# One row of one buffer stored on fifteen DMA engines: a layer-norm and GELU kernel bound by its transfers

## Chip, cores and metric

One core of a Trainium2 chip. The metric is the time of one execution on the device in microseconds (us), the median of several runs. The times compared here are of fast runs; label and label2 are single runs whose state is unknown, and are used for their traces alone. "Before" is the kernel as it stood, "the changed kernel" is it with the diff below. Engines in the profile: PE (TensorE), DVE (VectorE), ACT (ScalarE), POOL (GpSimd), SP (SyncE); "ACTq" and "SPq" are the sequencers of ACT and SP, where DMAs are issued. "DMA engine" is always one of the 16 that move data. No view of the profile numbers them. Numbers are names here: 15 ("the 16th") is the engine that gets no packet of the row from the transfer of 120 partitions, 0 and 1 are the two that get those of the transfers of two.

## Reference

```python
x: (8, 1024, 2048) float32; gamma, beta: (2048,)
normalized = (x - mean) / sqrt(var + eps)        # over the last axis
out = gamma * normalized + beta
return 0.5 * out * (1 + tanh(sqrt(2 / pi) * (out + 0.044715 * out ** 3)))
```

The input is 67.1 MB and so is the output. Each is moved once.

## The kernel before

The 8192 rows are cut into 16 buffers of 4 MB: 128 partitions, four rows of 8 KB each, which lie side by side in memory, so a partition's part of a buffer is one run of 32 KB. Five slots hold buffers. SP issues the loads; a load waits until the store that used its slot has landed. ACT issues the stores, a whole buffer at a time after its last row, the last buffer row by row.

```python
R = 4
SLOTS = 5
...
    xts = [sb(f"xt{s}", [P, R, d], f32) for s in range(SLOTS)]
...
    def slot(b):
        return (b + SLOTS - 1) % SLOTS
    def by_row(b):
        return b == B - 1
    def stored(b):
        return sum(16 * (R if by_row(c) else 1) for c in range(b) if slot(c) == slot(b))
...
            @block.sync
            def _(sy):
                for b in range(B):
                    s = slot(b)
                    if stored(b):
                        sy.wait_ge(s_store[s], stored(b))
                    ...
                    if b:
                        sy.dma_start(out=xts[s], in_=xg[b]).then_inc(s_load[s], 16)
...
            # ACT, for each row i after its GELU
                    if by_row(b):
                        ins.then_inc(s_r, 1)
                        ac.dma_start(out=og[b, :, q:q + 1], in_=xt[:, q:q + 1])._wait_ge(
                            s_r, b + q + 1).then_inc(s_store[slot(b)], 16)
                        ac.sem_inc(s_g, 1)
                    elif q == R - 1:
                        ins.then_inc(s_r, 1)
                        ac.dma_start(out=og[b], in_=xt)._wait_ge(s_r, b + 1).then_inc(s_store[slot(b)], 16)
                        ac.sem_inc(s_g, 1)
```

## Time and profile before

| | before |
|---|---|
| time, median of 3 runs | 319.68 us (319.67 to 319.75) |
| span in the profile | 317.8 us |
| moved | 134.27 MB, 423 GB/s in the mean |

These come from the page and the timed runs. The engines' sequences of packets are not a view of the profile: the trace holds a record of each packet (queue, start, duration, size) without the number of its engine, and I linked each packet to the one that starts where another ends, on the assumption, which no view shows, that every engine handles the packets of each transfer in order. For the kernel before this gives sixteen sequences of 348 packets each. The lines of the profile that carry the argument stand in the prediction.

### The profile page before, as it was taken

The numbers are of one execution on the slowest core, as the hardware profiler recorded it, in microseconds if no ns is written. First come the engines' busy times: TensorE is split into PE (matmuls) and PEld (weight loads), VectorE is DVE, ScalarE is ACT, GpSimd is POOL, SyncE is SP. The second block draws the span as 40 slices with busy tenths as digits, with TensorE's granted clock in tenths as the row PEclk, the third lists the DMA queues.
The fourth block names the chain that finished last, engine by engine and source line by source line (L and its number), as shares of the span: only waits on it lengthen the run. The fifth ranks groups of instructions, "written<-read, shape, count | busy, mean of one in ns | idle before, by whom it ended". The sixth has DMA issues, their size and how long they took to land.

```text
span 317.8 us, 2075 instructions
## 1 busy us (share of the span) xinstructions
PE 244.3 (77%) x520; PEld 57.1 (18%) x520; DVE 265.0 (83%) x514; ACT 253.9 (80%) x132; POOL 79.0 (25%) x73
## 2 busy tenths in 40 slices
PE   2769988888888898888877868598595895868810
PEld 1211222111212122211111111122121111112100
DVE  3499999999999999999969799696996969879500
ACT  2679999999999999999969779696995969968920
POOL 1033323232323231323213222231312213212000
DMA  7999999999999999999999999999999999999994
GB/s 291 438 462 396 459 396 445 412 454 404 458 400 459 422 437 445 412 450 408 458 417 441 437 421 454 404 458 412 450 433 425 450 408 450 408 458 421 437 404 206
DMA packets 5571, 134.27 MB, mean 423 GB/s; under 512 B 656, under 2 KB 704, under 8 KB 704
## 3 DMA queue, kind: packets, MB, share of 16 engines
q1 hardware_dynamic: 2736, 67.11, 49.4%
q10 hardware_dynamic: 2832, 67.13, 49.1%
q14 instruction: 3, 0.02, 0.0%
HBM read 67.13 MB, written 67.11 MB: 422 GB/s over the span
## 4 chain that ended last, share of the span: by engine, by line
DMA 44%; DVE 27%; ACT 19%; PE 3%; issue 2%; ACTq 1%; DVEq 0%; SPq 0%
DMA out_dram<-xt 27%; DVE sts L148 15%; DMA xt<-in_x_dram 15%; ACT yk L201 12%; DVE zg L164 9%; ACT xt L208 7%; PE ps L226 2%; DMA rows<-in_gamma_dram 2%; DVE mvs L157 2%; DVE nms L141 1%; ACTq L216 1%; DVE ves L158 1%; PE ps L243 1%; ACT g_t L197 1%; ACTq L211 0%
## 5 line engine op out<-in xcount | busy, mean ns | idle before, releaser
L148 DVE BATCH_NORM_STATS2 sts<-xt 128x6 f32<-128x512 f32 x256 | 163.5, 681 | 23.7 <-DMA xt<-in_x_dram 21.7
L201 ACT ACTIVATE yk<-xt,nms,rss 128x2048 bf16<-128x2048 f32 x64 | 134.1, 2095 | 41.7 <-DVE nms L141 41.2
L243 PE MATMUL ps<-zg,ident 128*128 128x512 bf16 x256 | 120.8, 627 | 50.9 <-DVE zg L164 50.9
L132 POOL TENSOR_TENSOR rss<-ves,mhalf 128x1 f32<-128x1 f32 x64 | 78.0, 1219 | 216.5 <-DVE ves L158 157.0
L239 PE MATMUL ps<-b_hl,ones_b 33*128 33x512 bf16 x256 | 120.6, 624 | 2.2 <-PEq L234 2.2
L208 ACT ACTIVATE xt<-ps 128x2048 f32<-128x2048 f32 x64 | 118.8, 1857 | 1.5 <-PE ps L243 1.5
L164 DVE TENSOR_TENSOR zg<-yk,g_t 128x2048 bf16<-128x2048 bf16 x64 | 78.0, 1218 | 5.0 <-ACT yk L201 3.0
L243 PEld LDWEIGHTS ps<-zg,ident 128*128 128x128 bf16 x256 | 27.6, 130 | 144.1 <-DVE zg L164 108.7
L239 PEld LDWEIGHTS ps<-b_hl,ones_b 33*128 33x128 bf16 x256 | 27.0, 127 | 92.1 <-issue 88.4
L157 DVE BATCH_NORM_AGGREGATE mvs<-sts 128x2 f32<-128x24 f32 x64 | 16.9, 264 | 2.2
L141 DVE TENSOR_SCALAR nms<-mvs,rss 128x1 f32<-128x1 f32 x64 | 12.6, 196 | 0.0
L226 PE MATMUL ps<-rows,ones 1*128 1x512 f32 x8 | 7.2, 1072 | 6.0 <-DMA rows<-in_gamma_dram 6.0
L158 DVE TENSOR_SCALAR ves<-mvs 128x1 f32<-128x1 f32 x64 | 9.8, 154 | 2.2
L194 ACT ACTIVATE b_hl<-rows 1x2048 bf16<-1x2048 f32 x1 | 1.9, 1909 | 4.9 <-DMA rows<-in_beta_dram 4.9
L226 PEld LDWEIGHTS ps<-rows,ones 1*128 1x128 f32 x8 | 2.5, 323 | 9.2 <-DMA rows<-in_gamma_dram 6.0
L172 DVE TENSOR_TENSOR b_hl<-rows,b_hl 1x2048 bf16<-1x2048 f32 x1 | 2.3, 2281 | 2.1 <-ACT b_hl L195 2.1
L197 ACT ACTIVATE g_t<-ps 128x2048 bf16<-128x2048 f32 x1 | 1.9, 1877 | 2.4 <-PE ps L226 2.4
L190 ACT ACT_TABLE_LOAD x1 | 1.3, 1283 | 0.9 <-SPq L106 0.9
L167 DVE MEMSET b_hl<- 33x1024 uint32 x1 | 0.9, 912 | 1.2 <-SPq L106 1.2
L195 ACT ACTIVATE b_hl<-rows 1x2048 bf16<-1x2048 f32 x1 | 1.9, 1908 | 0.0
L123 POOL MEMSET ones<- 65x128 f32 x1 | 0.2, 202 | 0.5 <-SPq L106 0.5
L127 POOL TENSOR_SCALAR_AFFINE_SELECT ident<-ident 128x128 bf16<-128x128 bf16 x1 | 0.3, 294 | 0.1
(7 smaller groups left out, 0.9 us busy)
## 6 DMA issues: line engine op xcount, KB each, us to landing
xt<-in_x_dram SPq DMA_DIRECT2D x15, 4096.0 KB, 24.3
out_dram<-xt ACTq DMA_DIRECT2D x15, 4096.0 KB, 37.0
xt<-in_x_dram SPq DMA_DIRECT2D x4, 1024.0 KB, 8.1
out_dram<-xt ACTq DMA_DIRECT2D x4, 1024.0 KB, 12.7
rows<-in_beta_dram ACTq DMA_DIRECT2D x2, 8.0 KB, 5.6
rows<-in_gamma_dram ACTq DMA_DIRECT2D x1, 8.0 KB, 5.0
```

The source lines that it names most:

```text
L132: po.tensor_tensor(out=rss[:, c], in0=ves[:, c], in1=mhalf, op=ALU.pow)._wait_ge(s_a, k + 1).then_inc(s_q, 1)
L141: ve.tensor_scalar(out=nms[:, c], in0=mvs[:, q, 0:1], scalar1=rss[:, c], scalar2=-1.0, op0=ALU.mult, op1=ALU.mult)._wait_ge(s_q, count).th ...
L148: ins = ve.bn_stats(out=sts[:, q, j, :], in_=xr[:, j, :])
L157: ve.bn_aggr(out=mvs[:, q], in_=sts[:, q])._wait_ge(s_o, count + 1).then_inc(s_o, 1)
L158: ve.tensor_scalar(out=ves[:, q:q + 1], in0=mvs[:, q, 1:2], scalar1=float(eps), scalar2=1.0, op0=ALU.add, op1=ALU.mult)._wait_ge(s_o, coun ...
L164: ve.tensor_tensor(out=zgs[q % 2], in0=yks[q % 2], in1=g_t, op=ALU.mult)._wait_ge(s_n, count).then_inc(s_z, 1)
L197: ac.activation(out=g_t, in_=pss[0], func=ACT.Identity)._wait_ge(s_tg, 1).then_inc(s_c, 1)
L201: ac.activation(out=yks[t % 2], in_=xts[slot(b)][:, q], func=ACT.Identity, scale=rss[:, q:q + 1], bias=nms[:, q:q + 1])._wait_ge(s_p, t + ...
L208: ins = ac.activation(out=xt[:, q], in_=pss[i % 2], func=ACT.Gelu_apprx_tanh)._wait_ge(s_t, i + 1)
L226: ins = pe.matmul(pss[0][:, cols(j)], lhsT=ones[64:65], rhs=rows[64:65, j * K // nsub:(j + 1) * K // nsub, :d // K], start=True, stop=True)
L239: ins = pe.matmul(ps[:, cols(j)], lhsT=ones_b, rhs=b_hl[:, cols(j)], start=True, stop=False)
L243: ins = pe.matmul(ps[:, cols(j)], lhsT=ident, rhs=zgs[k % 2][:, cols(j)], start=False, stop=True)
```

## The change

Its intent, as its words say: relieve the 16th DMA engine of one row of one buffer. Row 3 of buffer 7 is stored for partitions 0 to 119 in one transfer, and for the other eight in four transfers of two partitions. The first three rows of that buffer go in one store ahead of it. The diff also changes the last buffer: rows 0 and 1 go together, where each row had a store.

```diff
+LIGHT = 7
...
-    def by_row(b):
-        return b == B - 1
+    def stores(b):
+        every = slice(0, P)
+        if b == B - 1:
+            return [(0, 2, [every]), (2, 3, [every]), (3, 4, [every])]
+        if b == LIGHT:
+            return [(0, 3, [every]), (3, 4, [slice(0, 120)] + [slice(120 + a, P, 4) for a in range(4)])]
+        return [(0, R, [every])]
...
+                    for p in groups:
+                        ac.dma_start(out=og[b, p, lo:hi], in_=xt[p, lo:hi])._wait_ge(s_r, count).then_inc(
+                            s_store[slot(b)], 16)
+                    ac.sem_inc(s_g, 1)
```

The semaphore targets (`stored`) and the count of `s_r` follow from the same list.

More of the change, by code (lines that the diff above doesn't have):

```diff
@@ L98, in cols @@
         return slice(j * FMAX, (j + 1) * FMAX)
-    def by_row(b):
-        return b == B - 1
+    def stores(b):
[5 more added lines that the diff above has]
+        return [(0, R, [every])]
     def stored(b):
-        return sum(16 * (R if by_row(c) else 1) for c in range(b) if slot(c) == slot(b))
+        return sum(16 * len(p) for c in range(b) if slot(c) == slot(b) for _, _, p in stores(c))
     with tc.tile_critical(no_gpsimd_drain=True):
@@ L197, in _ @@
                 ac.activation(out=g_t, in_=pss[0], func=ACT.Identity)._wait_ge(s_tg, 1).then_inc(s_c, 1)
+                count = 0
                 for t in range(T + 1):
@@ L208, in _ @@
                     ins = ac.activation(out=xt[:, q], in_=pss[i % 2], func=ACT.Gelu_apprx_tanh)._wait_ge(s_t, i + 1)
-                    if by_row(b):
-                        ins.then_inc(s_r, 1)
-                        ac.dma_start(out=og[b, :, q:q + 1], in_=xt[:, q:q + 1])._wait_ge(
-                            s_r, b + q + 1).then_inc(s_store[slot(b)], 16)
-                        ac.sem_inc(s_g, 1)
-                    elif q == R - 1:
-                        ins.then_inc(s_r, 1)
-                        ac.dma_start(out=og[b], in_=xt)._wait_ge(s_r, b + 1).then_inc(s_store[slot(b)], 16)
-                        ac.sem_inc(s_g, 1)
-                    else:
-                        ins.then_inc(s_g, 1)
+                    ready = [g for g in stores(b) if g[1] == q + 1]
+                    if not ready:
+                        ins.then_inc(s_g, 1)
+                        continue
+                    count += 1
+                    ins.then_inc(s_r, 1)
+                    lo, hi, groups = ready[0]
+                    for p in groups:
+                        ac.dma_start(out=og[b, p, lo:hi], in_=xt[p, lo:hi])._wait_ge(s_r, count).then_inc(
+                            s_store[slot(b)], 16)
+                    ac.sem_inc(s_g, 1)
             @block.tensor
```

## The prediction

Four passages are cut from it where marked, because no run or trace of this case showed what they say: a paragraph on the number of engines in a transfer and on engines in general, how the odd transfers could come to run slowly, a fourth rival about instructions, and a word beside the last sign. That 120 partitions use 15 engines and two use two was assumed in steps 1 to 3.

> **What bounds the kernel now.** I read the page's DMA rows first, then its DMA queues, then the waits, the landings of the stores, and last the packet and semaphore records that lie under these views.
>
> The busy rows of the page, in 40 slices of 7.95 us:
>
> ```profile
> DVE  3499999999999999999969799696996969879500
> ACT  2679999999999999999969779696995969968920
> DMA  7999999999999999999999999999999999999994
> GB/s 291 438 462 396 459 396 445 412 454 404 458 400 459 422 437 445 412 450 408 458 417 441 437 421 454 404 458 412 450 433 425 450 408 450 408 458 421 437 404 206
> ...
> q1 hardware_dynamic: 2736, 67.11, 49.4%
> q10 hardware_dynamic: 2832, 67.13, 49.1%
> ```
>
> DVE and ACT are nearly full for the first half (digits of 9) and then show 6s and 7s; the DMA row is 9 from the second slice to the last but one. The two queues (loads, then stores; the columns are packets, MB and share of 16 engines' span) fill 98.5% together. So the transfers bound the kernel; compute has slack from half-way on. The waits of the load queue and of the rest say the same:
>
> ```profile
> DVE sts L148 <- DMA xt<-in_x_dram: 21.7, 8, 3.7
> ```
>
> ```profile
> SPq L119 <- DMA out_dram<-xt: 247.1, 11, 55.6
> ```
>
> The load queue waits 247 us for stores to free a slot, and DVE waits 21.7 us for loads. Nothing ahead of the DMA engines holds them up. At the end:
>
> ```profile
> 305.32 0.34 ACTq L211 DMA_DIRECT2D out_dram<-xt  x1
> ```
>
> This, from the timeline, is the issue of the last row's store. It lands at 316.5 us, 11.2 us later; the span ends at 317.8. The kernel ends when the slowest of the 16 engines has worked off its queue, and the shares above, being means over engines, cannot say by how much that one lags. The semaphore records can: each store counts 16, once for each engine. I read these times of its sixteen increments straight from the trace (us):
>
> ```
> buffer 0, issued  36.4: 14 engines 59.4 to 59.7,   then  59.9,  60.7
> buffer 6, issued 136.7: 14 engines 174.4 to 175.0, then 176.9, 178.3
> last row, issued 305.3: 14 engines 313.7 to 314.2, then 316.4, 316.5
> ```
>
> Two engines lag, not one. Linking each packet to the one that starts where another ends gives sixteen engines' sequences, without their numbers, about 8.39 MB each. None is left without a packet for more than about 0.3 us after 2 us. In the final rows an 8 KB packet follows the last every 0.306 us (26.8 GB/s), a 32 KB one takes 1.213 us. Fourteen sequences end at 313.3 to 313.9 us, two at 316.05 and 316.06. They lag for different reasons:
> - The **creeping engine** needs a mean of 1.2255 us for each 32 KB packet after 45 us where an ordinary engine needs 1.213; 213 such packets x 12.5 ns = 2.7 us. It falls behind steadily.
> - The **interrupted engine** is ordinary but for a few events. At 34.3 and at 99.5 us an 8 KB packet of the instruction queue takes 0.31 to 0.33 us, and the packet after it 1.875 and 1.744 us instead of 1.213: 0.32 + 0.66 + 0.31 + 0.53 = 1.8 us. Stretched packets at 60.4, 78.8 and 139.1 us (1.451, 1.347 and 1.395 us) add 0.24 + 0.13 + 0.18. In all 2.4 us, most of it before 140 us. (A third such fetch, at 109.9 us, seems to fall on another engine that ends 0.4 us late.)
>
> [...]
>
> **The change part by part.**
> 1. Row 3 of buffer 7 by 120 partitions: engine 15 (the 16th) is spared 8 packets of 8 KB, 8 x 0.306 = 2.45 us. The others keep their 8. This is just the lag of one of the two slow engines.
> 2. The other 8 partitions in four transfers of two: if each goes to engines 0 and 1, those get 4 packets more each, 4 x 0.306 = 1.22 us. If they are ordinary they end at 313.5 + 1.2 = 314.7 us, still ahead of a laggard's 316.06.
> 3. Buffer 7 in 24 KB and 8 KB pieces in place of 32 KB: 4 x 0.306 = 1.224 against 1.213 per partition, at most 8 x 0.011 = 0.09 us an engine; five more small semaphore packets of 9 ns on engines 0 and 1 (one more on the ordinary ones), under 0.05 us. The store of three rows is issued about a row (4.3 us) earlier than the whole was (153.4 us), but into a queue that already has work, since that buffer's store lands at 193.7 to 197.6 us: nothing gained.
> 4. The last buffer: rows 0 and 1 in one store instead of two. Row 0 was issued at 293.3 and waits until 297.6 now. The store of the buffer before, issued at 288.9, holds the engines to 303.9 us, so the delay is hidden. One semaphore packet and 8 packet boundaries fewer: less than 0.1 us gained.
> 5. ACT issues five more DMAs for buffer 7 and one fewer for the last: 4 x 0.34 = 1.4 us of its sequencer. ACT waits 41.2 us for DVE in all and the queues stay filled, so 0 on the path.
>
> Sum on the path: the 16th engine ends 2.4 us earlier if it is one of the two laggards. The end is then set by the other, at 316.05 instead of 316.06 us. The step 3 and 4 terms are within 0.1 us of each other. So I expect a gain of 0, give or take 0.2 us, out of a hoped-for 2.45, and 319.6 us (319.7 before, and 0.1 off for the one chance in six below).
>
> **The rivals.**
> - *The 16th engine is the only laggard that matters* (the change's intent). Then the end moves to the next slowest, engines 0 and 1 at about 314.7 us: 1.3 us earlier, 318.3 us. For it: the unprofiled runs might not have the second lag, if profiling makes it. Against: the profiled run took 319.58 us and the others 319.67 to 319.75, so the profile seems to add nothing; and both lags stand in the records of the last four stores. One chance in six.
> - *The extra packets fall on the other laggard*, that is, it is engine 0 or 1. Then it ends 1.22 us later, near 320.9 us. Nothing in the trace numbers the engines; with 2 of 15 engines, one chance in seven.
> - *The odd transfers run slowly*[...]. The disturbance would last as long as that row, 2.45 us at most, and hits engines with 2.2 us to spare, but the other laggard has none. Some tenths: 320.0 to 320.5 us. One in seven.
> - [...]
>
> **Range and chances.** The middle is no change, 319.7, set to 319.6 for the larger weight of the favourable side. The favourable rival gives 318.3 and the unfavourable 320.9; a range of 318.2 to 320.9 just holds both, and leaves out the gain of the whole 2.45 us (317.3) and two bad rivals at once, a tenth on each side. Two per cent is 6.4 us. To win that, all engines would have to move less data, and the bytes are the same; to lose it, the engines would have to run empty, and every queue has work waiting. So 0.98 for within 2%.
>
> **What would show it right or wrong.** Right: in the changed profile the last store still has a late increment, about 2.2 us behind the main group, but one in place of two; two engines end about 1.2 us after the ordinary ones; the last row's store is issued near 305.3 and the span is within 0.3 us of 317.8. Buffer 7's row has one 120-partition transfer with 15 increments by the DMA engines, and four with two. Wrong: all sixteen increments of the last store within 1.3 us of each other (the intent's gain), a last increment past 317 us (extra packets on the laggard), still two laggards as late as now (the 16th engine was neither), or more than 0.3 us of stretched packets around 195 us[...].

## The result, and the profile after

| | before | changed |
|---|---|---|
| time, median | 319.76 us (319.67 to 320.09, 6 runs) | 321.36 us (320.71 to 321.81, 6 runs) |
| ratio | | 1.0047, 95% interval 1.0034 to 1.0060 |
| span in the profile | 317.8 us | 319.3 us |
| last store's sixteen increments | 313.7 to 316.5 us | 314.8 to 318.0 us |

This ratio is the mean of the fast runs of one kernel over that of the other; the ratios of the experiments below come out of the fast runs of the same rounds without the first one, which was profiled. So they are not quite the ratios of the medians quoted. The change is 1.6 us slower. That is within 2%, as given 0.98, but above the range of 318.2 to 320.9.

The rows of the page of the changed kernel that answer to those of before:

```profile
DVE  3499999999999999999599899990596997969810
ACT  2679999999999999998599799991495996969960
...
DMA  7999999999999999999999999999999999999995
GB/s 293 433 452 427 428 402 447 406 452 423 435 447 407 448 419 443 443 415 447 415 443 439 417 449 397 416 390 431 427 447 431 431 423 431 447 435 423 423 414 223
...
q1 hardware_dynamic: 2736, 67.11, 49.4%
q10 hardware_dynamic: 2839, 67.13, 49.1%
```

The DMA row is as full as before and the bytes are the same, so the engines were not idle: some packets took longer. The GB/s row shows where: 397, 416 and 390 in the slices from 192 to 216 us (a slice is 8 us), where before has 454, 404 and 458. The number of packets on the store queue settles how the row was divided. It rose by 7, from 2832 to 2839. The data packets are as many as before; one store of 16 engines fewer in the last buffer takes away 16 small semaphore packets (656 for 41 transfers before), so the odd row added 23, which is 15 for the transfer of 120 partitions and 4 x 2 for the others, as the prediction assumed. (The trace has 39 packets of 4 bytes on that queue from 191 to 201 us: 16 of the three rows' store and these 23.)

The waits, for all engines and for the load queue:

```profile
DVE sts L155 <- DMA xt<-in_x_dram: 23.7, 6, 10.9
```

```profile
SPq L126 <- DMA out_dram<-xt: 247.5, 11, 54.9
```

The totals are hardly changed (21.7 and 247.1 us before). But one wait of DVE for a load is 10.9 us long, where 3.7 was the longest. The timeline tells which: the load of buffer 12 is issued when the store of buffer 7 has landed. In the changed kernel:

```profile
200.69 0.33 SPq L126 DMA_DIRECT2D xt<-in_x_dram  x1
```

and before:

```profile
197.66 0.33 SPq L119 DMA_DIRECT2D xt<-in_x_dram  x1
```

The buffer whose row was split lands 3 us later, although its first three rows were issued 4 us earlier. The issue of that row on ACT, in the changed kernel, with the issue of the last row of all:

```profile
153.76 3.23 ACTq L225 DMA_DIRECT2D out_dram<-xt  x5
...
310.06 0.34 ACTq L225 DMA_DIRECT2D out_dram<-xt  x1
```

Five issues took 3.23 us, 0.58 to 0.70 us each against 0.338 us for a store of 128 partitions (the two of 64 in halves7, below, took 0.55 and 0.60), and the last row's store comes at 310.1 us instead of 305.3.

Where did the 1.6 us come from? Busy time and GB/s in four stretches. The columns that matter are the last three: granted clock, DMA share, GB/s. Before:

```profile
186.00:196.00 10.00, 7.43 (x17) 1.73 (x18) 9.71 (x20) 9.24 (x6) 3.47 (x3) 1.00 1.04 449
196.00:201.00 5.00, 4.58 (x11) 1.18 (x12) 3.97 (x8) 4.28 (x3) 1.46 (x1) 1.00 1.05 452
201.00:208.00 7.00, 3.91 (x10) 0.92 (x9) 5.31 (x11) 4.27 (x3) 1.46 (x1) 1.00 0.93 403
208.00:216.00 8.00, 6.95 (x16) 1.56 (x15) 7.74 (x17) 7.29 (x4) 2.02 (x2) 1.00 1.03 442
```

Changed:

```profile
186.00:196.00 10.00, 8.20 (x18) 1.99 (x19) 9.74 (x20) 8.99 (x6) 3.12 (x3) 1.00 0.99 424
196.00:201.00 5.00, 4.58 (x11) 1.00 (x9) 4.93 (x10) 4.74 (x3) 1.46 (x1) 1.00 1.06 437
201.00:208.00 7.00, 6.17 (x15) 1.44 (x15) 6.86 (x14) 6.74 (x4) 2.92 (x2) 1.00 1.00 393
208.00:216.00 8.00, 6.97 (x16) 1.54 (x14) 7.70 (x16) 7.27 (x4) 1.64 (x2) 1.00 1.02 401
```

A packet counts whole where it starts, so a single stretch wobbles by some per cent (a share of 1.04 shows that). Over all 30 us it is 437 GB/s before and 413 after (each GB/s times its length, summed and divided by 30). The 24 GB/s that are missing over 30 us are 0.72 MB, which at 426 GB/s take 1.7 us: the whole loss of the kernel lies between 186 and 216 us.

The packet records show its form. After 45 us, a packet of 32 KB usually takes 1213 ns and one of 8 KB 309 ns. I call a packet stretched if it took over 50 ns more, and add up the excess over all engines. Before: 1.4 us. Changed: 25.5 us, 3.2 us of it in nine 8 KB packets of the odd row at 196.9 to 199.6 us (387 to 987 ns instead of 309), and 22.3 us in 52 packets of 32 KB, nearly all between 203 and 213 us. These are packets of ordinary transfers, the store of a later buffer and the load of buffer 12. Divided by 16 engines the 25.5 us are 1.6 us each.

In the linked sequences of the changed kernel the two with four more packets, engines 0 and 1, end last, at 317.7 and 316.9 us. The one without the row ends at 314.6 and takes 1.213 us for a 32 KB packet nearly throughout, so the 16th engine is neither the creeping nor the interrupted one. These two end at about 316.3 and 316.5, the rest between 314.5 and 316.0.

### The profile page after: what moved, and what is told of

Its sections match the earlier page's. It is cut to its first block, busy times and chain, and to the rows that moved or that the text cites. A ratio compares the mean times of both kernels' runs of the same rounds, so it can differ in the third digit from the quotient of the medians.

```text
span 319.3 us, 2079 instructions
## 1 busy us (share of the span) xinstructions
PE 244.3 (77%) x520; PEld 57.1 (18%) x520; DVE 265.0 (83%) x514; ACT 253.9 (80%) x132; POOL 79.1 (25%) x73
## 4 chain that ended last, share of the span: by engine, by line
DMA 45%; DVE 27%; ACT 19%; PE 3%; issue 2%; ACTq 1%; DVEq 0%; SPq 0%
DMA out_dram<-xt 27%; DMA xt<-in_x_dram 17%; DVE sts L155 16%; ACT yk L209 12%; DVE zg L171 9%; ACT xt L216 6%; PE ps L234 2%; DMA rows<-in_gamma_dram 2%; DVE mvs L164 2%; DVE nms L148 1%; ACTq L225 1%; DVE ves L165 1%; PE ps L251 1%; ACT g_t L204 1%; DVEq L185 0%
```

## The experiments

What is cut from the expectations below said which engines and partitions a transfer uses, or by what means packets would stretch; no run shows it. The theories, as they came up:
- **Theory 1, dry load queue:** the split row makes the store land late, the next load is issued late into an empty queue, and when loads come back all packets stretch.
- **Theory 2, heavy engines:** what costs is the four odd transfers on engines 0 and 1.
- **Theory 3, other division:** a row that isn't stored in one transfer of 128 partitions makes packets stretch. By what means was a guess of mine; no record shows which engine takes which partitions.
- **Theory 4, unequal loads:** packets stretch because engines have unequal work.
- **Theory 5:** theory 3 for the row itself; the later wave in ordinary 32 KB packets needs the late load as well.

All kernels but drop_eight gave the reference's result. The stretch is that of the one profiled run of each, which the ratio leaves out; runs of one kernel can differ by up to 5 us. halves7_late11 had one slow run of six, which is left out, and its interval reaches beyond 2%.

| kernel | median (us) | ratio | 95% interval | stretched 32 KB / 8 KB packets, us in all |
|---|---|---|---|---|
| before | 319.64 to 319.76 | 1 | | 1.4 / 0 |
| changed | 321.36 | 1.0047 | 1.0034 to 1.0060 | 22.3 / 3.2 |
| tail_only | 319.97 | 1.0008 | 0.9995 to 1.0022 | 0.9 / 0 |
| light7_old_tail | 321.37 | 1.0056 | 1.0042 to 1.0070 | 22.4 / 1.8 |
| split_only | 319.90 | 1.0007 | 0.9994 to 1.0021 | 7.6 / 0 |
| drop_eight | 320.27 | 1.0030 | 1.0017 to 1.0043 | 21.6 / 3.7 |
| one_of_eight | 320.86 | 1.0035 | 1.0022 to 1.0048 | 23.9 / 3.8 |
| late_load | 319.50 | 0.9999 | 0.9985 to 1.0012 | not used |
| late_load2 | 319.59 | 1.0005 | 0.9994 to 1.0017 | 1.5 / 0 |
| light14_old_tail | 320.64 | 1.0052 | 1.0031 to 1.0073 | 1.4 / 5.6 |
| split14 | 319.90 | 1.0006 | 0.9993 to 1.0019 | 0.8 / 0 |
| halves14 | 322.76 | 1.0099 | 1.0075 to 1.0124 | 10.4 / 17.1 |
| halves7 | 321.02 | 1.0041 | 1.0029 to 1.0053 | 21.5 / 0.4 |
| light12 | 320.94 | 1.0031 | 1.0017 to 1.0045 | 2.3 / 4.9 |
| halves12 | 322.10 | 1.0075 | 1.0061 to 1.0089 | 4.4 / 19.9 |
| light7_late11 | 324.90 | 1.0161 | 1.0145 to 1.0177 | 40.7 / 6.0 |
| halves7_late11 | 326.15 | 1.0205 | 1.0164 to 1.0245 | 30.8 / 11.2 |

### Taking the change apart: tail_only, light7_old_tail, split_only

tail_only: `LIGHT = -1`, so that only the last buffer's stores change.

> Only the last buffer's stores are changed (rows 0 and 1 together). Theories 1 and 2: 319.7 us, within 0.2, as the engines work on the store before until 304 us. Rival (the tail is what costs): above 320.5 us, with engines without work after 293 us.

Measured 319.97 us, the interval holds 1. The merged rows cost nothing that shows, as the prediction said.

light7_old_tail is the rest:

```diff
-            return [(0, 2, [every]), (2, 3, [every]), (3, 4, [every])]
+            return [(q, q + 1, [every]) for q in range(R)]
```

> The change without its second part: buffer 7 as in the changed kernel, the last buffer in four stores as before. Theories 1 and 2: as the changed kernel, 321.4 us within 0.5. Rival (the tail costs): below 320.5.

321.37 us, as the changed kernel. The whole loss is in buffer 7.

split_only takes the odd partitions out, too (old tail from here on):

```diff
-            return [(0, 3, [every]), (3, 4, [slice(0, 120)] + [slice(120 + a, P, 4) for a in range(4)])]
+            return [(0, 3, [every]), (3, 4, [every])]
```

> Buffer 7 is stored as three rows and one row, both with all 128 partitions; the tail is that of before. Theory 1 (dry load queue): the packets of 24 KB and 8 KB take turns one for one with the loads' 32 KB packets, so the store falls behind and the loads get ahead; the store lands after 198.5 us, the load that needs its slot is issued late, no load is in the queues for some us, and when loads come back packets on all engines stretch, above 1 us on each: 320.3 to 321.4 us. Theory 2 (heavy engines): what costs is the odd transfers on engines 0 and 1; without them 319.7 us, within 0.2.

319.90 us; four runs at 319.68 to 320.14, one, the profiled one, at 321.06. In that trace the load of buffer 12 is issued at 200.0 us, nearly as late as in the changed kernel, and no load packet starts from 198 to 203 us. So the first half of theory 1 is right, in this trace: 24 KB and 8 KB packets fall behind the loads' 32 KB ones, and the split alone delays the landing (load issued at 200.0 us, 197.7 before). That the packets take turns was counted in the changed kernel: 227 of 282 steps from one packet to the next between 178 and 196 us change the queue. Yet four of the five runs lose nothing that shows: 0.2 us in ratio, which leaves out the profiled run (with it 0.5 us). The split alone is not the cost in most runs; in one it came with a third of the stretch and 1.4 us.

### Which part of the odd row: drop_eight, one_of_eight

drop_eight gives a wrong result: `(3, 4, [slice(0, 120)])`, and the last eight partitions of the row are not stored.

> Wrong on purpose: row 3 of buffer 7 is stored for partitions 0 to 119 alone, the other 8 not at all. Light without heavy. Theory 1: as split_only or the changed kernel, 319.9 to 321.2. Theory 2: 319.7 to 319.9 us; and no gain below 319.4, since the trace of the changed kernel has the 16th engine among the ordinary ones.

one_of_eight stores them in one transfer: `(3, 4, [slice(0, 120), slice(120, P)])`.

> Buffer 7 as in the changed kernel, but the other 8 partitions in one transfer[...] in place of four; tail of before. Theory 1 alone: the split and the dry load queue stay, 319.9 to 321.2 us as far as the stretch on all engines goes. Theory 2: 0.31 us more on eight engines and no engine with four more: as split_only, 319.9 us within 0.3.

Against split_only's 1.0007, the transfer over fifteen engines alone has 1.0030, with the eight in one transfer 1.0035, in four 1.0056 (light7_old_tail). So about 0.7 us of the 1.8 come from storing 120 partitions on 15 engines, 0.2 from the other eight in one transfer and 0.7 more from cutting that into four. This division is rough: the intervals overlap at each step, two of the four ran in other rounds on another chip, and with the changed kernel's 1.0047 in place of 1.0056 the last step is 0.4 us. Theory 2 covers at most that last part: drop_eight has no heavy engine and has the same 22 us of stretched 32 KB packets. It is slower than before, although the 16th engine has 2.45 us less to do there and no engine has more.

### Is it the dry load queue: late_load, late_load2

The kernel before with one more wait in SP's loop. All transfers are unchanged:

```diff
                         sy.wait_ge(s_store[s], stored(b))
+                    if b == 12:
+                        sy.wait_ge(s_p, 40)
```

> The kernel before, with one more wait: the load of buffer 12 also waits until the 40th mean is ready, about 203.4 us instead of 197.7. All transfers and instructions on ACT are those of before. Theory 1: no load is in the queues for a few us around 202 to 205, packets on all engines stretch when it comes, the end moves by 1 to 1.7 us, to 320.7 to 321.4. Theory 2: the DMA engines still have stores, nothing is lost, 319.7 us within 0.2.

A miss of mine: I had miscounted the rows, the wait was over before it could hold, and the load was issued at 197.1 us. The run is only a control. late_load2 has 44 in place of 40.

> As late_load, where the wait was over before it could hold anything, but for the 44th mean: the load of buffer 12 is issued near 203.4 us instead of 197.7. Theory 1 (a dry load queue, then packets that stretch on all engines when loads come back): some us without load packets between 200 and 206, mean extra packet time per engine 0.4 us (as in the profiled run of split_only) to 1.4 us (as in the changed kernel), and the end moves by as much: 320.1 to 321.2 us. Theory 2 (the odd transfers' engines): 319.7 us within 0.2, no stretched packets.

The load of buffer 12 is now issued at 203.9 us, later than in the changed kernel, and no load packet starts from 201 to 207 us. The time is 319.59 us (five runs at 319.44 to 319.72, one at 320.75), and the stretch is 1.5 us, as before. The same stretches as above, for late_load2:

```profile
186.00:196.00 10.00, 7.41 (x16) 1.72 (x16) 9.67 (x20) 9.24 (x6) 3.47 (x3) 1.00 1.02 439
196.00:201.00 5.00, 4.29 (x10) 1.14 (x11) 4.29 (x9) 4.60 (x3) 1.46 (x1) 1.00 1.05 452
201.00:208.00 7.00, 3.89 (x10) 0.86 (x8) 4.96 (x11) 3.92 (x3) 1.46 (x1) 1.00 0.94 407
208.00:216.00 8.00, 6.95 (x16) 1.56 (x15) 7.74 (x15) 7.50 (x4) 2.02 (x2) 1.00 1.04 451
```

Weighted, that is 437 GB/s, just what before has. A late load into an empty queue stretches no packets here, and theory 1 as stated falls. But it isn't free. The store of buffer 14 is issued later than before, at 294.5 us instead of 288.9:

```profile
294.48 0.34 ACTq L218 DMA_DIRECT2D out_dram<-xt  x1
```

and by the packet records up to 14 of the 16 engines have no packet between 294.1 and 295.4 us, 1.1 us each in the mean. So the ordinary engines end at about 315.1 us instead of 313.5. The time hides this, because the last engine ends at 315.9 us, about where the laggards of before do. The changed kernel has hardly any such gap (0.1 us an engine between 200 and 300 us).

### The row where no load runs: light14_old_tail, split14, halves14

`LIGHT = 14`, whose store is issued after the last load has landed.

> The same lightening in buffer 14, after the last load, with the tail of before. Theory 1: no load queue to run dry, no stretch on all engines, so the ordinary engines end near 313.6 us as before; engines 0 and 1 get 1.2 us of packets and perhaps as much of stretch in the odd ones, 314.8 to 316.3; end by the two old laggards or those: 319.5 to 320.2 us. If the 16th engine were a laggard and the other not, 318.3. Theory 2: the odd transfers cost wherever they stand: 320.8 to 321.5 us.

320.64 us, between the two theories (four runs at 320.45 to 320.65, two at 322.3 and 322.5). There is no wave in 32 KB packets, but the row's own packets stretch, 5.6 us in all. The creeping engine can be followed here from 60 us on by its slow packets: it does store the odd row, so it is not the 16th, and it ends at 317.05 us, last of all, with 1.1 us of stretch in 8 KB packets. The heavy engines end at 315.0 and 316.5.

Now the control and the test that was to separate division from load. split14 is split_only in buffer 14. halves14 stores row 3 in two transfers of 64 partitions. I took it that every engine gets the same 8 packets as in split14:

```diff
-            return [(0, 3, [every]), (3, 4, [every])]
+            return [(0, 3, [every]), (3, 4, [slice(0, 64), slice(64, P)])]
```

> Control for halves14: buffer 14 stored as three rows and one, both with 128 partitions. No load follows. 319.7 us within 0.3, no stretched packets at 296 to 307 us.

> Row 3 of buffer 14 in two transfers of 64 partitions[...]. Theory 3[...]: the row's packets stretch by over 0.2 us an engine in the mean, as in light14_old_tail (0.4), and the time is 320.1 to 320.8 us. Theory 4 (unequal loads are what stretches packets): no stretch, as split14, 319.7 us within 0.3.

split14: 319.90 us, no stretched 8 KB packet. halves14: 322.76 us, 51 stretched 8 KB packets with 17 us in all. The stretch of time in which the row runs, split14 first, then halves14:

```profile
302.00:308.00 6.00, 1.60 (x4) 0.30 (x2) 0.00 (x0) 2.04 (x2) 0.00 (x0) 1.00 1.01 426
```

```profile
302.00:308.00 6.00, 4.48 (x10) 0.85 (x8) 1.23 (x1) 4.52 (x3) 0.00 (x0) 1.00 1.00 352
```

In both the engines are busy all the time (share 1.01 and 1.00), but 352 instead of 426 GB/s come out. If the loads per engine are equal, as I took them to be, theory 4 isn't needed: what differs is how the row is divided. How this stretches packets is not shown, and no single factor stands out: 22 of the 51 stretched packets took 1.9 to 2.1 times the usual 0.309 us, but 11 took more than 2.2 times, up to 4.4. (Another caveat: in halves14's profiled run, the slowest of its six, some loads of earlier buffers stretched as well, 10 us in all, and its times spread from 321.8 to 324.6, so the 2.9 us over split14 are not all the row's.)

### The row beside loads: halves7, light12, halves12

halves7 is halves14 in buffer 7.

> The same two halves in buffer 7, loads beside it. Theory 3: stretched packets in the row and a wave after it as in drop_eight (1.5 us an engine), 320.3 to 321.3 us. Theory 4: as split_only, 319.9 us within 0.3, with at most 0.5 us of stretch an engine.

321.02 us: two halves, and nearly the loss of the changed kernel. The stretch lies in the later 32 KB packets (21.5 us), hardly in the row's own (0.4 us). Buffer 12's store is also issued beside running loads, but no later load waits for its slot.

> The light row in buffer 12, stored near 250 us: loads run beside it, but no later load waits for that slot. Tail of before. If the wave of stretched 32 KB packets after the row in buffer 7 needs a load that starts late into an empty queue with engines out of step (theory 5): no wave after 255 us beyond 0.2 us an engine; the row's own stretch stays, the end is set by a laggard or engines 0 and 1 at 319.9 to 320.7 us. If the odd row alone makes the wave (theory 3 in full): 1 us an engine or more between 250 and 290 us, 320.9 to 321.8 us.

> Two halves of row 3 in buffer 12[...]. Theory 5: no wave, 319.7 to 320.3 us. Theory 3 in full: a wave as in halves7 (1.3 us an engine) and 320.7 to 321.4 us.

There was no wave: in the two traces the 32 KB packets stretch by 2.3 and 4.4 us, not 20. But this doesn't test theory 5, for the row came to its turn only after 281 us, when the last load was over: both runs repeat light14_old_tail and halves14, and a row beside loads for which no load waits was not seen. The time of halves12 misses theory 5's forecast (322.1 instead of 319.7 to 320.3), for I had not counted the row's own stretch. In halves12, 22 of the row's 33 stretched packets took more than 2.2 times their usual duration, up to 4.6. Five engines end at 317.5 to 318.5 us, the others at 314.1 to 316.0.

### Moving the load of buffer 11: light7_late11, halves7_late11

To keep the load queue from running empty after the odd row, the load of buffer 11 waits as well (`if b == 11: sy.wait_ge(s_p, 40)`, in light7_old_tail and halves7).

> light7_old_tail, but the load of buffer 11 waits for the 40th mean, so that it starts near 184 us instead of 177 and is still under way when the load of buffer 12 is issued near 200: the load queue is not empty after the odd row (it is empty for some us before it, when engines are in step). Theory 5: no wave of stretched 32 KB packets (under 5 us in all instead of 22), 320.0 to 320.8 us. Theory 3 in full (the row alone makes the wave): 321.2 us or more.

> The same for halves7 (321.02 us). Theory 5: no wave, 319.7 to 320.3 us. Theory 3 in full: 20 us of stretched 32 KB packets in all and 321 us.

Both missed badly, 324.90 and 326.15 us, and not as a clean refutation: holding the load from 177 to 183.8 us gave the stores the engines to themselves, so the odd row ran earlier, at 186 us, just as the loads came back. In that order the damage is largest (30 to 41 us of stretched 32 KB packets), and the engines no longer swing together. Before, 13 to 16 of them load at one moment and store at the next; here about eight load and eight store at any time, with stretched packets up to 290 us. So the largest damage came where loads begin on top of the odd row. Two runs are missing: the held load of buffer 11 without an odd row, which would tell whether holding it is bad by itself, and the row with loads that never stop, which would test theory 5.

### Numbering the engines: label, label2

Row 3 of buffer 14 in many transfers of 15, 14, ... 1 partitions, which were to give each engine another number of packets:

```diff
+            ends = [0]
+            for k in (15, 14, 13, 12, 11, 10, 9, 8, 8, 7, 6, 5, 4, 3, 2, 1):
+                ends.append(ends[-1] + k)
+            return [(0, 3, [every]), (3, 4, [slice(u, v) for u, v in zip(ends, ends[1:])])]
```

> Row 3 of buffer 14 is stored in sixteen transfers of 15, 14, ... 1 partitions and one more of 8[...]. Slower by some us through the issues; only the numbers matter. From light14_old_tail, where the engine without the row was an ordinary one: neither the creeping nor the interrupted engine is number 15, nor 0 or 1. If the creeping one is 15 after all, the reading of the sequences is wrong.

323.0 us: all packets have 8 KB, many overlap, and the sequences could not be linked to the end. label2 cuts each transfer of k partitions into two pieces of columns, the first of 256 x k bytes, so that the size names the transfer.

> A second try to number the engines: in row 3 of buffer 14 each transfer of k partitions (15 down to 1) is cut into two pieces of columns whose sizes belong to that k alone, so the packets of transfer k are known by their size. [...] Expected: none of the two laggards is number 15, 0 or 1.

It took 332.7 us, for 31 issues, which doesn't matter here. The starts of the first pieces, from the packet records (us):

```
k=15: 301.32 301.32 301.34 301.43 301.45 301.48 301.49 301.58 301.58 301.61 301.64 301.66 301.86 304.23 304.34
k=14: 301.66 301.78 301.80 301.82 301.90 301.91 301.96 301.98 301.98 302.06 302.08 302.18 304.55 304.66
k=7:  304.23 304.58 304.96 305.56 306.37 307.90 309.00
k=6:  304.55 304.91 305.88 306.75 308.22 309.32
k=5:  305.63 306.21 307.17 308.54 309.64
k=4:  307.48 307.54 307.76 308.87
k=3:  307.95 308.44 308.62
```

Both laggards, 2.4 us behind, are among the 15 engines of the first transfer, and still among seven: here too the engine that the transfer of 15 leaves out is no laggard. On each, the next transfer's packet comes 0.32 to 0.33 us after the last (307.90, 308.22, 308.54, 308.87 and 309.00, 309.32, 309.64). The second chain has no packet in the transfer of four, the first none in that of three. If an engine's number is the size of the largest transfer listed that has no packet for it, the laggards are numbers 4 and 3. That the other engines can be ordered so was not shown. The numbers hold for this run, on chip 7; no run numbers the laggards of the profiled before, whose chip the record doesn't give. The second laggard isn't the same in every run: in tail_only the creeping engine ends at 316.0 us, but the interrupted one already at 314.8, and the kernel is no faster.

If they are the same elsewhere, they also tell why I ran no better version: of the transfers listed, only that of three partitions has no packet of either laggard's chain. As an estimate from the numbers above: to spare thirteen engines two packets each (0.61 us), three engines would take 26 packets, 8.7 each or 2.65 us, and end at 313.5 + 2.65 = 316.15 us, later than the laggards' 316.06. One packet each could gain 0.3 us at most, less than the stretch that such transfers bring.

## Why the prediction was wrong

**What held.** The bound: the queues were full, and ACT's five issues of the odd row, longer than I had counted (3.23 us together, against 1.4 for the whole change), did not show in the time. The division by packets, 15 and 4 x 2. The tail: no effect (tail_only). That lightening the 16th engine gains nothing held too, but not for the reason I gave. I let it be one of the two laggards, with the other setting the end; in the trace of the changed kernel it is neither. (drop_eight, which only lightens, can't test the reason: its packets stretch by 25 us.)

**The step that failed** is the one in which packets keep their durations: "those get 4 packets more each, 4 x 0.306 = 1.22 us", and "at most 8 x 0.011 = 0.09 us an engine" for the pieces. In the odd row nine 8 KB packets took 0.39 to 0.99 us instead of 0.306, and around the row and after it all engines together lost 25.5 us, 1.6 us each. This is the size of the loss.

**The rival that came true was mis-sized.** "The odd transfers run slowly" had the effect. I bounded it by the row's own 2.45 us and by "some tenths", and gave it one chance in seven. That dividing the row otherwise costs time is shown: each of halves14's six runs is 1.9 us or more above split14's median. By what means, and that the loads are equal there, is not shown. In buffer 7 most of the stretch was outside the row: 22.3 of 25.5 us in later, ordinary packets. My sign for it, more than 0.3 us of stretched packets around 195 us, did appear, mostly some 10 us later. Another sign came true for a reason that isn't the one I gave: the last increment is at 318.0 us, past 317, but the extra packets fell on two ordinary engines, not on a laggard.

**"Nothing gained" by the earlier issue** hid a second error in step 3. The store lands later, not at the same time, because its smaller packets take turns with loads of 32 KB (in the linked sequences 227 of 282 steps from one packet to the next between 178 and 196 us change the queue); the slot's next load came 3 us late. In late_load2 and in four of split_only's five runs this by itself didn't show in the time.

**The heavy engines.** I had them at 314.7 us, "still ahead of a laggard's 316.06". In the linked sequences they end at 317.7 and 316.9 and set the end. Cutting the eight partitions into four transfers is worth 0.4 to 0.7 us of the loss (one_of_eight against the changed kernel and light7_old_tail; the intervals overlap).

**What stays open:** why ordinary 32 KB packets stretch 5 to 15 us after the row in buffer 7. They did so in every kernel with a row divided otherwise there (21.5 to 40.7 us). They did not with the late load alone (late_load2); the split alone had a third of it in one run (split_only); light12 and halves12 can't tell, as no loads were left. That both are needed fits these, but the test made for it broke down. And an odd row isn't needed for every such wave: in the kernel before, 17 load packets stretch by 9 us in all at 37.9 to 40.1 us, soon after the first store is issued, and every kernel here has the like. I had left that stretch out by counting from 45 us on.

## What to carry to other kernels

Before work is taken off a slow DMA engine, number the engines: transfers on 15, 14, 13, ... engines with sizes of their own showed it in one run, though one run's laggards need not be another's. A row in transfers of fewer partitions did not run here as the same row in one of 128 (halves14's packets took up to 4.4 times the usual 0.309 us, split14 had none stretched): take packet times from a run, and compare with a control of the same bytes. Where the queues are full, look in the packet durations for lost time, not in idle shares (halves14 moved 352 GB/s at a share of 1.00, split14 426 at 1.01).
